# A hybrid decoder layer on one core: queries and first key/value columns of the in-projection by seven block products, compression moved into the convolution stage

## The chip, the cores and the metric

One core of one Trainium2 chip. The metric is the device time of one execution in microseconds (us). Engines: TensorE (PE, with its weight loads PEld), VectorE (DVE), ScalarE (ACT), GpSimd (POOL) and SyncE (SP), whose queue issues most transfers.

## The reference

One layer on x of 1024 tokens by 1024 columns, in fp32. A token mixer (sparse attention with three branches, and a gated short convolution) and an MLP:

```
h = rms_norm(x, g_mix_norm)
z = h @ w_in                                   # 1024 x 2840
q, kc, vc, ks, vs, kw, vw, gates, hc, cg, bg = split(z)
        # q 512 columns; kc, vc, ks, vs, kw, vw 128 each; gates 24; hc, cg, bg 512 each
k_cmp = rms_norm(gelu(blocks(kc) @ w_cmp1[0] + b) @ w_cmp2[0] + b)     # "compression"
v_cmp =          gelu(blocks(vc) @ w_cmp1[1] + b) @ w_cmp2[1] + b
attn  = gated sum of attention on (k_cmp, v_cmp), on selected blocks (ks, vs), in a window (kw, vw)
conv  = bg * causal_conv3(cg * hc)
x = x + [rms_norm(attn), rms_norm(conv)] @ w_o
x = x + square(relu(rms_norm(x) @ w_up)) @ w_down
```

## The kernel before

Every fp32 product is three passes of TensorE (`mm3`, L636): high times high, high times low, low times high. The high half of an operand is a copy by ScalarE (`copy_act`, L629), the low half a subtraction, mostly by VectorE. One matmul has a 128x128 stationary operand and 512 moving columns (280 or 256 in places) and sums into a bank of PSUM.

The stages, in the order of the program:

- **Front.** `x_in` (L748) loads x transposed in 16 pieces of 128x512 (256 KB), scales and splits them; `norm_in` loads x again for the norms of the tokens. `z_tokens` (L801) multiplies tokens (stationary) by columns of w_in: first 512 columns kc, vc, ks, vs of all eight token blocks, then the 512 columns of q, then 280 columns (kw, vw, gates). That is 8 (blocks of 128 rows of w_in) x 8 (token blocks) x 3 passes = 192 matmuls for each of the three; the first two together are the 384 of 512 columns. `token_sums` (L821) makes sums of blocks of x that the convolution stage needs, `late_sum` (L831) one more. Keys are normed (`k_norm`) and written to DRAM turned; q likewise.
- **Compression.** `compress_steps` (L880) is a generator; between the q matmuls one step at a time is taken: load the blocks of kc or vc from DRAM (`ch`), turn them (`tp`), split them (`ah`, `al`; the latter on POOL), load w_cmp1 in eight pieces (`w1r`), split each (`w1h`, `w1l`), 96 matmuls in all into `hp`, then gelu, a turn and the second product.
- **Convolution.** `channels` (L1054) already computes a 2x2 block product with seven products, not eight (Strassen's way in Winograd's form): A11, S1, S2, A12, S3, S4, A22, each with a block of x or a sum of such (`b11`, `t1`, `t2`, `b21`, `b12`, `b22`, `t4`), summed in three chains of banks X, W, Z. `u_pair` (L1092) and the loop after it evaluate them and convolve.
- **Output projection of the convolution part** (`wc` matmuls), keys, scores and values of the attention, the rest of w_o, and an MLP whose products are by seven as well.

All of this is recorded into `Plan` (L156) and written out at the end: a list scheduler (`schedule`, `latest`) gives each instruction a rank from the longest work behind it and orders each engine's queue; `shaken` (L565) shakes the ranks with the numbers in `SEEDS` (L153), and the best of its orders by its own costs is issued (`best`, `issue`). So all instructions have the line L273 of the issuing helper, and are told apart by tile names. `plan.plus`, `plan.slack`, `plan.drag` and `plan.follow` move the rank of single operations. PSUM has eight banks: three of the pool psP (L700; "pt") and five of psB (L702; "mm"). In each engine's queue instructions run in order; a transfer in SP's queue waits with all behind it until its tile is free.

Of the kernel before, what the change touches and what calls it, by code (L numbers as in the profile page):

```python
# [19 lines left out]
P = 128  # L20
# [4 lines left out]
H = 8  # L25
# [21 lines left out]
C_CONV = C_GATE + 3 * H  # L47
GELU_C = 0.7978845608028654
# [104 lines left out]
SEEDS = (174, 96, 16, 293, 242, 303, 622, 488, 681, 529, 552, 868, 906, 858, 745, 812, 849, 989, 1138, 1111, 1227, 1330, 1240, 1619, 1452, 1751, 1854, 1808, 1969, 2299, 2182, 2463, 2584, 3018, 3202, 4890, 5120, 5678, 5748, 5759, 5732, 5809, 5825, 6181, 6472, 6446, 6357, 6538, 6828, 7002, 7139, 7387, 7641, 7905, 7699, 8110, 8891, 9541, 9548, 9753, 9890, 10201, 10211, 10442, 12007, 13133, 13704, 13855, 13990, 15390, 15367, 15624, 15886, 16292, 16730, 16933, 17091, 17166, 17516, 17595, 17935, 17801, 17972, 18997, 19783, 20400, 21422, 23298, 24412, 24583, 24684, 25041, 25935, 26634, 27058, 30527, 37332, 43721, 44172, 45465, 56150, 69531, 71323, 73032, 73374, 78977, 79699, 84172, 87695, 92708, 93300, 98646, 99114, 99374, 120984, 125933, 126536, 137741, 144395, 147541, 152192, 155111, 155792, 163960, 208317, 212893, 221248, 221764,)  # L153


class Plan:  # L156
# [450 lines left out]
def trunk_layer(ctx, tc, x, x_t, vectors, w_in, g_qk, w_cmp1, b_cmp1, w_cmp2, b_cmp2,  # L607
# [79 lines left out]
    ht_stack = ExitStack()  # L687
    htp = pool(ht_stack, "htp")
    b_stack, wp_stack = ExitStack(), ExitStack()
    twp = pool(b_stack, "twp", side="right")  # L690
    hTh = [(twp, htp)[i].tile([P, KD, 512], F32R, name=f"hTh{i}") for i in range(2)]
    hTl = [(twp, htp)[i].tile([P, KD, 512], F32R, name=f"hTl{i}") for i in range(2)]

    kcn = twp.tile([P, 2 * HD], F32, name="kcn")
    g_bc = twp.tile([P, 4, HD], F32, name="g_bc")
    gq_bc, gk_bc = g_bc[:, 0], g_bc[:, 1:]
    TD = {n: [htp.tile([P, 4, 512], F32R, name=f"{n}{q}") for q in "hl"] for n in ("t1", "t2")}
    wp = pool(wp_stack, "wp", bufs=4, side="right")
    psP_stack = ctx.enter_context(ExitStack())
    psP = pool(psP_stack, "psP", bufs=3, space=PSUM, side="right")  # L700
    psB_stack = ExitStack()
    psB = pool(psB_stack, "psB", bufs=5, space=PSUM)  # L702

# [30 lines left out]
    b1 = ExitStack()
    zt = pool(b1, "zt", bufs=2, side="right")
    xp_stack = ExitStack()
    xp = pool(xp_stack, "xp", side="right")

    def quarter(i, j):
        return [a[j][:, 4 * i:4 * i + 4] for a in (hTh, hTl)]  # L740

    TD["b11"], TD["b12"], TD["b21"], TD["b22"] = quarter(0, 0), quarter(0, 1), quarter(1, 0), quarter(1, 1)

    def x_part(k, th):
        q = f"{k // 4 + 1}{th + 1}"
        return [xT[q][:, k % 4]] + [a[:, k % 4] for a in TD["b" + q]]

    def x_in(k, th):  # L748
        raw, hi, lo = x_part(k, th)
# [5 lines left out]

    def norm_in(tb):
        xt = xp.tile([P, D], F32, name="xt") if tb % 2 else zt.tile([P, D], F32, name="xt", tag="qn", bufs=1)
# [3 lines left out]
        rsqrt(rmix[:, tb:tb + 1], ss, 1, 1.0 / D)  # L761

    plan.plus = 200.0
    nc.scalar.dma_start(cols, vectors)
    tp = psP.tile([P, 512], F32, name="warm", tag="pt")
# [4 lines left out]
    kv_pieces, last = [], []  # L770
    for j in range(4):
        if j:
            for k in (2 * j, 2 * j + 1):
                x_in(k, 0)
            kv_pieces.append(w_piece(wiv[:, 2 * j:2 * j + 2, C_KV:C_KV + 512], [P, 2, 512], lo_eng=nc.vector))
            continue
        raw = wp.tile([P, 2, 512], F32, name="w_raw", bufs=2)
        kv_pieces.append((wp.tile([P, 2, 512], F32R, name="w_hi"), wp.tile([P, 2, 512], F32R, name="w_lo")))
        for k in range(2):
            x_in(k, 0)  # L780
            hi, lo = [a[:, k] for a in kv_pieces[0]]
            nc.sync.dma_start(raw[:, k], wiv[:, k, C_KV:C_KV + 512])
            if k:
                copy_act(hi, raw[:, k])
            else:
                nc.vector.tensor_copy(hi, raw[:, k])
            tt(nc.vector, lo, raw[:, k], hi.bitcast(F32), ALU.subtract)
    for tb in range(4):
        norm_in(tb)
    for k in range(KD):  # L790
        x_in(k, 1)
    for tb in range(4, NT):
# [6 lines left out]
    tt(nc.vector, gk_bc, gk_bc, gq_bc.unsqueeze(1).to_broadcast([P, 3, HD]), ALU.mult)  # L799

    def z_tokens(pieces, tbs, n, steps=iter(()), per=0):  # L801
        pss = [psB.tile([P, 512], F32, name="zp", tag="mm") for _ in tbs]
        for j, (wh, wl) in enumerate(pieces):
            for ps, tb in zip(pss, tbs):
                t = slice((tb % 4) * P, (tb % 4 + 1) * P)
                for i in range(2):
                    k = 2 * j + i
                    mm3(ps[:, :n], hTh[tb // 4][:, k, t], hTl[tb // 4][:, k, t], wh[:, i], wl[:, i],
                        k == 0, k == KD - 1)
            for _ in range(per):  # L810
                plan.plus = 12
                next(steps, None)
                plan.plus = 0.0
        return list(zip(tbs, pss))

    def split_sum(o, k, raw):
        hi, lo = [a[:, k] for a in TD[o]]
        copy_act(hi, raw)
        tt(nc.vector, lo, raw, hi.bitcast(F32), ALU.subtract)

    def token_sums():  # L821
        for k in range(4):
            x11, x12, x21, x22 = [xT[n][:, k] for n in ("11", "12", "21", "22")]
            tt(nc.vector, x11, x12, x11, ALU.subtract)
            split_sum("t1", k, x11)
            tt(nc.vector, x22, x22, x11, ALU.subtract)
            split_sum("t2", k, x22)
            tt(nc.vector, x21, x21, x22, ALU.subtract)
            split_sum("t4", k, x21)

    def late_sum(tp_, o, p, m):  # L831
        f = {n: [a.bitcast(F32) for a in TD[n]] for n in (m, p)}
        for k in range(4):
            (ah, al), (bh, bl) = [[a[:, k] for a in f[n]] for n in (m, p)]
            a, b = [tp_.tile([P, 512], F32, name=n, bufs=1) for n in ("ta", "tb")]
            tt(nc.vector, a, bh, ah, ALU.subtract)
            tt(nc.vector, b, bl, al, ALU.subtract)
            tt(nc.vector, a, a, b, ALU.add)
            split_sum(o, k, a)

    token_sums()
    with b1:
        def k_norm(src, br, tb):
            dst = zt.tile([P, 2, G, 32], F32, name="krow")
            sq = zt.tile([P, HD], BF16, name="ksq", bufs=2)
            ss = st.tile([P, G], F32, name="kss")
            for g in range(G):
                c = slice(g * HD, (g + 1) * HD)
                nc.scalar.activation(sq, src[:, c], AF.Square, accum_out=ss[:, g:g + 1])
            ri = st.tile([P, G], F32, name="kri")  # L850
            rsqrt(ri, ss, G, 1.0 / HD)
            for g in range(G):
                nc.vector.scalar_tensor_tensor(dst[:, :, g], src[:, g * HD:(g + 1) * HD].rearrange("p (j d) -> p j d", j=2),
                                               ri[:, g:g + 1], gk_bc[:, br].rearrange("p (j d) -> p j d", j=2),
# [1041 lines left out]
```

## Time and profile before

| | |
|---|---|
| median of 3 runs | 1188.5 us (1187.66 to 1188.91) |
| the profiled execution | 1187.4 us, its span 1185.6 us |
| busy share of the span | PE 99%, PEld 82%, DVE 77%, ACT 59%, POOL 61% |
| matmuls, transposes included | 5766 |
| instructions of DVE, ACT, POOL | 1827, 1550, 663 |
| read from and written to HBM | 111.87 and 48.23 MB |

How to read it: busy times are sums of single instructions. Matmuls overlap, so the duration of one (0.39 us for 512 columns) is longer than what it occupies TensorE; that is read from the starts of neighbours, or from how many start in a stretch. The granted clock (PEclk) is given in tenths of full speed; 9 is 90% or more.

### The profile page before, as it was taken

What the parts mean: (1) busy time and instruction counts of PE and PEld (TensorE: products, weight loads), DVE (VectorE), ACT (ScalarE), POOL (GpSimd) and SP (SyncE); (2) the same over time, 40 slices, a digit from 0 to 9 for tenths busy, and PEclk for the clock granted to TensorE, in tenths of its full rate; (3) what the DMA queues carried; (4) which work ended last, traced back from release to release, by engine and by line L of the source; (5) the groups of instructions that cost most, each with busy time, mean ns of one, the idle gap of its engine ahead of it and who ended that gap; (6) DMA issues with size and microseconds to landing.
All of it is one profiled execution on the core that took longest, in us unless ns stands there. A gap on an engine that the chain in (4) does not pass through costs nothing.

```text
span 1185.6 us, 18003 instructions
## 1 busy us (share of the span) xinstructions
PE 1173.6 (99%) x5766; PEld 977.4 (82%) x5766; DVE 908.0 (77%) x1827; ACT 698.3 (59%) x1550; POOL 722.9 (61%) x663
## 2 busy tenths in 40 slices
PE   9999999999999999999999999999999999999998
PEld 7888978888878888888788888888888888888887
DVE  8868968696799999998876555554479979887875
ACT  7868634362599988889764555546335444444441
POOL 1444400013356554535878977877799899888971
PEclk9999999999999999999999999999999999999999
DMA  9745581245121101104055535353469545553513
GB/s 341 194 138 169 154 153 50 68 162 171 53 64 46 61 12 63 55 19 143 18 178 186 167 127 187 121 182 121 163 230 389 149 137 178 162 167 102 174 46 142
DMA packets 115102, 161.28 MB, mean 136 GB/s; under 512 B 21472, under 2 KB 68960, under 8 KB 115008
## 3 DMA queue, kind: packets, MB, share of 16 engines
q1 hardware_dynamic: 108752, 152.44, 40.4%
q10 hardware_dynamic: 5520, 5.28, 1.3%
q0 software_dynamic: 736, 2.43, 0.7%
q8 instruction: 45, 0.74, 0.3%
q14 instruction: 49, 0.40, 0.1%
HBM read 111.87 MB, written 48.23 MB: 135 GB/s over the span
## 4 chain that ended last, share of the span: by engine, by line
PE 90%; DVE 4%; ACT 3%; DMA 1%; issue 1%; SPq 0%; ACTq 0%; DVEq 0%
PE X L273 29%; PE Z L273 18%; PE zp L273 8%; PE zX L273 5%; PE ot L273 5%; PE tp L273 5%; PE wc L273 4%; PE W L273 4%; PE wa L273 3%; PE zZ L273 3%; PE zW L273 1%; DVE pl L273 1%; DMA w1r<-in_w_cmp_dram 1%; DVE pt L273 1%; PE hp L273 1%
## 5 line engine op out<-in xcount | busy, mean ns | idle before, releaser
L273 PE MATMUL X<-we,uu 128*128 128x512 f32 (+1 forms) x726 | 201.0, 388 | 0.0
L273 PE MATMUL Z<-we,uu 128*128 128x512 f32 (+1 forms) x576 | 166.2, 388 | 0.0
L273 PEld LDWEIGHTS X<-we,uu 128*128 128x128 f32 x726 | 136.0, 188 | 28.2 <-DVE y L273 0.2
L273 ACT ACTIVATE uu<-ur 128x512 fp32r<-128x512 f32 x108 | 67.2, 630 | 123.4 <-PE Z L273 70.9
L273 PEld LDWEIGHTS Z<-we,uu 128*128 128x128 f32 x576 | 107.9, 188 | 22.3
L273 ACT ACTIVATE pt<-pt,nm 128x640 f32<-128x640 f32 (+7 forms) x128 | 93.7, 734 | 39.7 <-DVE nm L273 39.4
L273 DVE TENSOR_TENSOR y<-X,y 128x512 f32<-128x512 f32 x129 | 86.8, 682 | 32.5 <-PE X L273 31.4
L273 POOL TENSOR_TENSOR d<-d 128x512 f32<-128x512 f32 x64 | 98.0, 1551 | 9.9 <-DVE d L273 8.3
L273 DVE TENSOR_TENSOR pl<-tp,ph 128x512 fp32r<-128x512 f32 (+1 forms) x148 | 95.0, 654 | 3.6 <-ACT ph L273 3.2
L273 PE MATMUL tp<-ident,pt 128*128 128x128 f32 x528 | 91.2, 273 | 0.0
L273 ACT ACTIVATE ph<-tp 128x512 fp32r<-128x512 f32 (+1 forms) x148 | 80.8, 573 | 11.3 <-PE tp L273 8.9
L273 POOL TENSOR_TENSOR uu<-ur,uu 128x512 fp32r<-128x512 f32 x54 | 80.9, 1502 | 5.0 <-ACT uu L273 4.9
L273 ACT ACTIVATE we<-s 128x512 fp32r<-128x512 f32 x55 | 34.7, 631 | 83.6 <-PE Z L273 46.8
L273 DVE TENSOR_TENSOR y<-Z,y 128x512 f32<-128x512 f32 x96 | 64.9, 681 | 21.6 <-PE Z L273 21.2
L273 PEld LDWEIGHTS tp<-ident,pt 128*128 128x128 f32 x528 | 66.0, 141 | 10.7 <-DVE pl L273 0.6
L273 POOL MEMSET Qz<- 64x512 f32 x16 | 8.3, 520 | 106.0 <-PE zZ L273 104.5
L273 PE MATMUL zp<-w_hi,hTh 128*128 128x512 f32 (+1 forms) x192 | 64.6, 365 | 0.4 <-ACT hTh L273 0.4
L273 PE MATMUL zp<-w_lo,hTh 128*128 128x512 f32 (+1 forms) x192 | 64.8, 363 | 0.0
L273 PE MATMUL zp<-w_hi,hTl 128*128 128x512 f32 (+1 forms) x192 | 64.1, 360 | 0.0
L273 DVE TENSOR_TENSOR we<-wu,we 128x512 fp32r<-128x512 f32 x38 | 43.4, 1153 | 26.0 <-PE X L273 16.6
L273 POOL TENSOR_TENSOR we<-wd,we 128x512 fp32r<-128x512 f32 x32 | 48.0, 1501 | 24.7 <-ACT we L273 24.3
L273 POOL TENSOR_TENSOR pt<-pt,rr 128x640 f32<-128x640 f32 (+4 forms) x64 | 62.3, 1001 | 0.0
(1353 smaller groups left out, 3608.0 us busy)
## 6 DMA issues: line engine op xcount, KB each, us to landing
u_d<-d SPq DMA_DIRECT2D x112, 256.0 KB, 3.6
ur<-u_d SPq DMA_DIRECT2D x108, 256.0 KB, 2.8
wu<-in_w_up_dram SPq DMA_DIRECT2D x16, 1024.0 KB, 5.9
wd<-in_w_down_dram SPq DMA_DIRECT2D x16, 1024.0 KB, 6.9
xt<-in_x_dram SPq DMA_DIRECT2D x10, 512.0 KB, 5.6
x<-in_x_t_dram SPq DMA_DIRECT2D x16, 256.0 KB, 6.6
w1r<-in_w_cmp_dram SPq DMA_DIRECT2D x16, 256.0 KB, 2.8
q_d<-qn SPq DMA_DIRECT2D x8, 512.0 KB, 3.5
```

The lines of the kernel that those rows point to most:

```text
L273: node.do.append(lambda: getattr(engine, method)(*[real(x) for x in a], **{k: real(x) for k, x in kw.items()}))
```

## The change

The q columns (512) and the columns kc, vc, ks, vs (512) become the two halves of one 1024x1024 block product with the seven products of the convolution stage: weights A11, A12 (q and kv columns of the rows, in halves) and sums S1 to S4, tokens in the sums that the convolution needs anyway, all of which are now made at the start (`late_sum` goes). Each product is 4 x 4 x 3 = 48 matmuls; seven are 336 in place of 384. The 280 columns come first (`rest_tokens`). Compression is advanced inside the convolution's products (`advance`, two steps after each product from the third on), and what is left of it runs before the first output gate. The tiles of the convolution's output and the loads of keys (`kn`) move behind that. PSUM has, until the attention, four banks in rotation, one "m5" (compression's `hp`, `cps`, late chains W) and three of a pool ps0. New ranks: 152 numbers, some of which shake a narrower stretch.

```
-SEEDS = (174, 96, 16, 293, ...)
+SEEDS = (186, 36, 24000136, 238, 1000267, ...)
...
         a, w, size, how = r.uniform(0, 700), r.uniform(5, 40), r.choice((.5, 1, 2, 5)), r.random()
+        if seed >= 1000000:
+            a, w = seed // 1000000 * 10 + r.uniform(-5, 10), r.uniform(1, 15)
...
+    def bank(name, fifth=False):
+        return psB.tile([P, 512], F32, name=name, tag="m5" if fifth else "mm", bufs=1 if fifth else 4)
+    def banks(name, outer):
+        if not outer:
+            return [bank(name) for _ in range(4)]
+        return [ps0.tile([P, 512], F32, name=name, tag=t, bufs=n) for t, n in (("pt", 1), ("r2", 2), ("r2", 2))] + [bank(name, True)]
...
+    def rest_tokens(th):
+        pss = banks("zp", th == 0)
+        for k in range(KD):
+            bh, bl = TD[f"b{k // 4 + 1}{th + 1}"]
+            for j, ps in enumerate(pss):
+                t = slice(j * P, (j + 1) * P)
+                mm3(ps[:, :280], bh[:, k % 4, t], bl[:, k % 4, t], rest[0][:, k], rest[1][:, k], k == 0, k == KD - 1)
...
+    def product(name, b, chain, first, ready):
+        if first:
+            Z[chain] = banks("z" + chain, chain == "X")
+        bh, bl = TD[b]
+        for k in range(4):
+            ready(k)
+            raw = W[name, k]
+            hi, lo = [wr.tile([P, 512], F32R, name=f"w{q}", bufs=HL) for q in "hl"]
+            copy_act(hi, raw)
+            tt(nc.vector, lo, raw, hi.bitcast(F32), ALU.subtract)
+            if name == "S2":
+                a12 = W["S4", k] = W["A12", k]
+                tt(nc.gpsimd, a12, a12, raw, ALU.subtract)
+            for j, ps in enumerate(Z[chain]):
+                t = slice(j * P, (j + 1) * P)
+                mm3(ps, bh[:, k, t], bl[:, k, t], hi, lo, first and k == 0, k == 3, skip_group_check=True)
...
+    def sums_k(k):
+        a11, a21, a22 = W["A11", k], w_in_k("A21", 0, k, w_tile("c")), w_in_k("A22", 1, k, w_tile("d"))
+        tt(nc.vector, a11, a11, a21, ALU.subtract)
+        tt(nc.vector, a21, a21, a22, ALU.add)
+        tt(nc.vector, a22, a22, a11, ALU.subtract)
+        W["S3", k], W["S1", k], W["S2", k] = a11, a21, a22
...
+    product("A12", "b21", "W", True, lambda k: w_in_k("A12", 1, k, w_tile("b")))
+    t0 = kept("X", 0, x_tile, "t0")
+    product("S2", "t2", "X", False, sums_k)
+    for tb in range(4):
+        kv_out(tb, Z["W"][tb], t0[tb])
...
+    product("S1", "t1", "Z", True, lambda k: None)
+    t1 = kept("X", 1, w_tile("d"), "t1")
+    product("S3", "b12", "X", False, lambda k: None)
+    za = kept("Z", 1, w_tile("c"), "za")
+    product("S4", "b22", "Z", False, lambda k: None)
+    for tb in range(4, NT):
+        q_out(tb, Z["X"][tb - 4], za[tb - 4])
+    product("A22", "t4", "X", False, lambda k: w_in_k("A22", 1, k, w_tile("a")))
+    for tb in range(4, NT):
+        kv_out(tb, Z["Z"][tb - 4], t1[tb - 4])
+    wr_stack.close()
+    for tb in range(4):
+        q_out(tb, Z["X"][tb])
...
+        def advance():
+            done.append(None)
+            if len(done) > SKIP:
+                plan.plus = 12
+                for _ in range(STEPS):
+                    next(steps, None)
+                plan.plus = 0.0
...
                 if chain not in ps:
-                    ps[chain] = psB.tile([P, 512], F32, name="z" + chain, tag="mm")
+                    ps[chain] = bank("z" + chain, chain == "W" and len(done) > 14)
...
                 yield name, ps[chain]
+                advance()
...
+            if c == 0:
+                for _ in steps:
+                    pass
+                cp_stack.close()
+                zt_stack.close()
+                mcp = pool(b2, "mcp", side="right")
+                MCh, MCl = [mcp.tile([P, 4, T], F32R, name=f"MC{q}") for q in "hl"]
```

Counted over the whole program, TensorE has 48 matmuls 128x512 less and nothing else changed; VectorE has 30 operations on two tensors 128x512 more, 12 fused ones (scale and add), 8 of 280 columns, and 7 of 1024 and 4 of 560 columns less; ScalarE 27 of 512 and 8 of 280 more, 7 of 1024 and 4 of 560 less; POOL 4 subtractions 128x512 more; SP 18 transfers of 512 and 8 of 280 columns more, 7 of 2x512 and 4 of 2x280 less.

SP's queue at the start of the program, before (w_raw are columns kc to vs of w_in, x the transposed input):

```order
L273 DMA w_raw<-in_w_in_dram 128x512
L273 DMA x_184<-in_x_t_dram 128x512
L273 DMA w_raw<-in_w_in_dram 128x512
L273 DMA x_184<-in_x_t_dram 128x512
L273 DMA w_raw<-in_w_in_dram 128x2x512
```

and after (wk are rows of the 280 columns):

```order
L275 DMA x_162<-in_x_t_dram 128x512
L275 DMA x_163<-in_x_t_dram 128x512
L275 DMA x_164<-in_x_t_dram 128x512
L275 DMA x_165<-in_x_t_dram 128x512
L275 DMA wk<-in_w_in_dram 128x280 x2
L275 DMA x_166<-in_x_t_dram 128x512
```

A first weight piece and a first x piece were the first two transfers; now four x pieces precede the first weight piece.

VectorE's queue of the change around the first low half of A12 (wl_185, from wA12_308), with buffer numbers (x11 to x22 are blocks of x and their sums, wA11 and wA21 weights and their sums, t2l the low half of a sum, krow and kturn the keys of the window, g_bc the norm's factors):

```order
L275 TENSOR_TENSOR wA11_192<-wA11_192,wA21_370 128x512
L275 TENSOR_TENSOR t2l_642<-x11_162,t2h_469 128x512
L275 TENSOR_SCALAR rs_t_614<-kss_610 128x2
L275 TENSOR_SCALAR rs_t_593<-kss_579 128x2
L275 TENSOR_TENSOR x11_165<-x22_177,x11_165 128x512
L275 STREAM_TRANSPOSE kturn_773<-krow_671 128x128
L275 TENSOR_TENSOR x21_169<-x21_169,x11_165 128x512
L275 TENSOR_SCALAR gates_65<-ge_607 128x12
L275 TENSOR_TENSOR wl_185<-wA12_308,wh_190 128x512
L275 SCALAR_TENSOR_TENSOR krow_827<-z_650,kri_653,g_bc_207 128x2x32 x2
L275 TENSOR_TENSOR wl_804<-wA12_329,wh_808 128x512
```

Before, the second group of weights needed only its own split on VectorE; sums of x stood beside it and sums of weights did not exist. Now both stand ahead of the low half.

TensorE's queue where the compression's hidden products (hp, from pieces w1h, w1l and blocks ah, al) stand, before (zp are projection matmuls):

```order
L273 MATMUL zp<-w_lo,hTh_126 128x512
L273 MATMUL hp<-w1h,ah_742 128x256
L273 MATMUL hp<-w1l,ah_742 128x256
L273 MATMUL zp<-w_hi,hTh_126 128x512
L273 MATMUL zp<-w_lo,hTh_126 128x512
L273 MATMUL zp<-w_hi,hTl_125 128x512 x2
L273 MATMUL zp<-w_hi,hTh_126 128x512 x2
```

and after (zX, a chain of the convolution; r, the turn of the tokens' norm factors):

```order
L275 MATMUL zX<-b12l,wcuh 128x512
L275 MATMUL hp<-w1h,ah_1691 128x256
L275 MATMUL hp<-w1l,ah_1691 128x256
L275 MATMUL zX<-b12h,wcul 128x512
L275 MATMUL zX<-b12h,wcuh 128x512
L275 MATMUL r_1650<-ident,bc 128x128
L275 MATMUL hp<-w1h,al_1690 128x256
```

The hidden products have moved from among the projection's matmuls to among the convolution's.

## Rows read from the trace of the kernel before

**Rows 1.** The page: busy time, share and instructions of each engine; VectorE's busy tenths and the granted clock in 40 slices of the span.

```profile
PE 1173.6 (99%) x5766; PEld 977.4 (82%) x5766; DVE 908.0 (77%) x1827; ACT 698.3 (59%) x1550; POOL 722.9 (61%) x663
...
DVE  8868968696799999998876555554479979887875
...
PEclk9999999999999999999999999999999999999999
```

**Rows 2.** Busy time by stretch: the stretch, its length, then busy time and instructions started of PE, PEld, DVE, ACT and POOL, granted clock, share of the DMA engines, GB/s.

```profile
5.00:10.00 5.00, 4.58 (x19) 3.44 (x18) 3.31 (x6) 2.96 (x5) 0.00 (x0) 1.00 0.98 342
8.00:60.00 52.00, 51.98 (x224) 42.10 (x225) 46.63 (x100) 42.84 (x99) 18.32 (x27) 1.00 0.87 274
66.00:137.00 71.00, 69.14 (x436) 61.36 (x435) 58.22 (x127) 50.92 (x206) 34.36 (x29) 1.00 0.53 158
137.00:160.00 23.00, 22.27 (x104) 17.88 (x103) 19.08 (x55) 12.20 (x36) 7.85 (x10) 1.00 0.58 141
160.00:260.00 100.00, 100.00 (x438) 80.64 (x437) 79.72 (x127) 46.08 (x80) 4.78 (x9) 1.00 0.35 79
310.00:345.00 35.00, 32.45 (x191) 25.69 (x190) 34.65 (x110) 33.40 (x85) 17.23 (x27) 1.00 0.26 76
345.00:560.00 215.00, 214.93 (x1327) 185.70 (x1327) 200.91 (x679) 187.26 (x432) 117.49 (x184) 1.00 0.17 57
560.00:1180.00 620.00, 618.25 (x2752) 509.85 (x2751) 432.65 (x539) 302.66 (x559) 509.04 (x345) 1.00 0.47 158
```

**Rows 3.** The chain of work that ended last, in order of time: start, length, what (x: instructions in one piece).

```profile
8.02 58.46 PE zp L273 x251
66.83 0.76 PE tp L273 x7
...
96.17 0.60 PE hp L273 x5
...
117.30 4.63 PE zp L273 x36
...
257.75 5.74 PE wc L273 x24
```

**Rows 4.** Groups of TensorE's matmuls from 66 to 137 us, shapes apart: line, operation, output from inputs, shape, count, then busy time and mean ns of one, then idle time just before them and what ended it.

```profile
L273 PE MATMUL zp<-w_hi,hTl 128*128 128x512 f32 x45 | 16.7, 399 | 0.0
L273 PE MATMUL zp<-w_lo,hTh 128*128 128x512 f32 x43 | 16.4, 402 | 0.0
L273 PE MATMUL zp<-w_hi,hTh 128*128 128x512 f32 x42 | 16.1, 397 | 0.0
L273 PE MATMUL zp<-w_hi,hTh 128*128 128x280 f32 x59 | 15.3, 293 | 0.0
L273 PE MATMUL zp<-w_lo,hTh 128*128 128x280 f32 x59 | 15.2, 293 | 0.0
L273 PE MATMUL zp<-w_hi,hTl 128*128 128x280 f32 x57 | 14.4, 291 | 0.0
L273 PE MATMUL hp<-w1l,ah 128*128 128x256 f32 x32 | 9.2, 288 | 0.8 <-DVE w1l L273 0.6
L273 PE MATMUL hp<-w1h,ah 128*128 128x256 f32 x32 | 9.2, 287 | 0.9 <-ACT w1h L273 0.9
L273 PE MATMUL hp<-w1h,al 128*128 128x256 f32 x32 | 9.0, 281 | 0.0
L273 PE MATMUL tp<-ident,ch 128*128 128x128 f32 x16 | 2.9, 272 | 0.0
```

**Rows 5.** TensorE's instructions in order of time at the start: start, length, engine, instruction, count, and in brackets the idle time before it and what ended it (the first six projection matmuls, and the first of the unbroken run).

```profile
5.34 1.22 PE L273 MATMUL zp<-w_hi,hTh 128*128 128x512 f32 x2
...
7.21 0.39 PE L273 MATMUL zp<-w_hi,hTl 128*128 128x512 f32 x1
8.02 0.50 PE L273 MATMUL zp<-w_hi,hTh 128*128 128x512 f32 x1 [0.41 <-ACT hTh L273]
```

**Rows 6.** ScalarE's instructions in order of time: the splits of the first and second x piece.

```profile
4.57 0.72 ACT L273 ACTIVATE hTh<-x,cols 128x512 fp32r<-128x512 f32 x1 [1.87 <-DMA x<-in_x_t_dram]
...
7.24 0.72 ACT L273 ACTIVATE hTh<-x,cols 128x512 fp32r<-128x512 f32 x1 [1.43 <-DMA x<-in_x_t_dram]
```

**Rows 7.** VectorE's instructions in order of time, several of one kind on one row: the length is from the first's start to the last's end.

```profile
5.33 0.75 DVE L273 SCALAR_TENSOR_TENSOR hTl<-x,cols,hTh 128x512 fp32r<-128x512 f32 x1 [0.39 <-ACT hTh L273]
...
10.82 4.73 DVE L273 SCALAR_TENSOR_TENSOR hTl<-x,cols,hTh 128x512 fp32r<-128x512 f32 x7
15.45 1.28 DVE L273 TENSOR_SCALAR x<-x,cols 128x512 f32<-128x512 f32 x3
...
30.54 0.48 DVE L273 SCALAR_TENSOR_TENSOR krow<-z,kri,g_bc 128x64 f32<-128x64 f32 x2
...
33.39 1.89 DVE L273 TENSOR_TENSOR x<-x,x 128x512 f32<-128x512 f32 x3
```

**Rows 8.** Groups of VectorE's instructions from 160 to 260 us, columns as in rows 4: the low halves of the convolution's weights, and an evacuation of a chain X.

```profile
L273 DVE TENSOR_TENSOR wcul<-wcr,wcuh 128x512 fp32r<-128x512 f32 x29 | 19.7, 684 | 3.3 <-PE zX L273 1.6 <-PE zZ L273 1.2 <-ACT wcuh L273 0.5
...
L273 DVE TENSOR_TENSOR ca<-zX,ca 128x512 f32<-128x512 f32 x5 | 3.4, 690 | 10.5 <-PE zX L273 10.5
```

**Rows 9.** The page's costliest groups, columns as in rows 4: low halves of the MLP's weights on VectorE and on POOL.

```profile
L273 DVE TENSOR_TENSOR we<-wu,we 128x512 fp32r<-128x512 f32 x38 | 43.4, 1153 | 26.0 <-PE X L273 16.6
...
L273 POOL TENSOR_TENSOR we<-wd,we 128x512 fp32r<-128x512 f32 x32 | 48.0, 1501 | 24.7 <-ACT we L273 24.3
```

More of the change, by code (lines that the diff above doesn't have):

```diff
@@ L47 @@
 C_CONV = C_GATE + 3 * H
+HL = 5
+SKIP, STEPS = 2, 2
 GELU_C = 0.7978845608028654
@@ new lines, in kept @@
+    def kept(chain, th, tile, name):
+        out = []
+        for j, ps in enumerate(Z[chain]):
+            t = tile(name)
+            copy_act(t, ps, scale=rmix[:, 4 * th + j:4 * th + j + 1])
+            out.append(t)
+        return out
+    def sums_k(k):
[4 more added lines that the diff above has]
+        W["S3", k], W["S1", k], W["S2", k] = a11, a21, a22
@@ new lines, in k_norm @@
+    def k_norm(src, br, tb):
+        dst = zt.tile([P, 2, G, 32], F32, name="krow")
+        sq = zt.tile([P, HD], BF16, name="ksq", bufs=2)
+        ss = st.tile([P, G], F32, name="kss")
+        for g in range(G):
+            c = slice(g * HD, (g + 1) * HD)
+            nc.scalar.activation(sq, src[:, c], AF.Square, accum_out=ss[:, g:g + 1])
+        ri = st.tile([P, G], F32, name="kri")
+        rsqrt(ri, ss, G, 1.0 / HD)
+        for g in range(G):
+            nc.vector.scalar_tensor_tensor(dst[:, :, g], src[:, g * HD:(g + 1) * HD].rearrange("p (j d) -> p j d", j=2),
+                                           ri[:, g:g + 1], gk_bc[:, br].rearrange("p (j d) -> p j d", j=2),
+                                           op0=ALU.mult, op1=ALU.mult)
+        turned = zt.tile([P, G * HD], F32, name="kturn", bufs=1)
+        nc.vector.transpose(turned, dst.rearrange("p j g d -> p (j g d)"))
+        nc.sync.dma_start(k_d[br - 1][tb * P:(tb + 1) * P], turned)
@@ new lines, in q_out @@
+    def q_out(tb, ps, t=None):
+        z = zt.tile([P, 512], F32, name="z") if t is None else t
+        if t is None:
+            copy_act(z, ps, scale=rmix[:, tb:tb + 1])
+        else:
+            nc.vector.scalar_tensor_tensor(z, ps, rmix[:, tb:tb + 1], t, op0=ALU.mult, op1=ALU.add)
+        sq = zt.tile([P, HD], BF16, name="qsq", tag="ksq", bufs=2)
+        ss = st.tile([P, H], F32, name="qss", bufs=2)
+        for h in range(H):
+            c = slice(h * HD, (h + 1) * HD)
+            nc.scalar.activation(sq, z[:, c], AF.Square, accum_out=ss[:, h:h + 1])
+        ri = st.tile([P, H], F32, name="qri", bufs=2)
+        rsqrt(ri, ss, H, 1.0 / HD)
+        tt(nc.vector, ri, ri, qscale, ALU.mult)
+        qn = zt.tile([P, G, 4, R, 32], F32R, name="qn", bufs=1)
+        zh = z.rearrange("p (h d) -> p h d", h=H)
+        tt(nc.vector, zh, zh, ri.unsqueeze(2).to_broadcast([P, H, HD]), ALU.mult)
+        zT = zt.tile([P, 512], F32, name="zT", bufs=1)
+        nc.vector.transpose(zT, z)
+        for g in range(G):
+            zg = zT[:, g * 256:(g + 1) * 256].rearrange("p (r c t) -> p c r t", r=R, c=2)
+            hi, lo = qn[:, g, 2 * g:2 * g + 2], qn[:, g, 2 - 2 * g:4 - 2 * g]
+            copy_act(hi, zg)
+            tt(nc.vector, lo, zg, hi.bitcast(F32), ALU.subtract)
+        nc.sync.dma_start(q_d[tb * P:(tb + 1) * P], qn.rearrange("p g c r t -> p (g c r t)").bitcast(F32))
@@ L769, in trunk_layer @@
     plan.plus, plan.cold = 0.0, False
[L770 to L787, printed above, removed]
+    last = []
+    for k in range(KD):
+        x_in(k, 0)
+        rest_in(k)
     for tb in range(4):
[L789 to L792, printed above, removed]
         norm_in(tb)
@@ L799, in trunk_layer @@
     tt(nc.vector, gk_bc, gk_bc, gq_bc.unsqueeze(1).to_broadcast([P, 3, HD]), ALU.mult)
[L801 to L805, printed above, removed]
+    rest_tokens(0)
+    for k in range(KD):
+        x_in(k, 1)
+    for tb in range(4, NT):
+        norm_in(tb)
+    rest_tokens(1)
@@ new lines, in trunk_layer @@
+    for n in ("t2", "t1", "t4"):
+        operand(n)
+    product("A11", "b11", "X", True, lambda k: w_in_k("A11", 0, k, w_tile("a")))
+    for k in range(4):
+        x11, x12, x21, x22 = [X[n, k] for n in ("11", "12", "21", "22")]
+        tt(nc.vector, x22, x22, x12, ALU.subtract)
+        tt(nc.vector, x12, x12, x11, ALU.subtract)
+        tt(nc.vector, x11, x22, x11, ALU.add)
+        split_sum("t2", k, x11)
+        tt(nc.vector, x21, x21, x11, ALU.subtract)
+        split_sum("t1", k, x12)
+        split_sum("b12", k, x22)
+        split_sum("t4", k, x21)
@@ L806, in z_tokens @@
                 for i in range(2):
                     k = 2 * j + i
[L808 to L839, printed above, removed]
```

396 lines of the change are left out of this document (177 added, 219 removed).

## The prediction

> **What bounds the kernel now.** I read the busy times and the slices first, then busy times by stage, then the chain that ended last, and single instructions at last. TensorE is busy 99% of the span at full granted clock in every slice [rows 1]. So the time is the length of TensorE's queue, and what counts is how long each matmul occupies it, start to start, not its pipelined duration (0.39 us). By stage [rows 2]: from 8 to 60 us 224 matmuls of 512 columns start in 52.0 us, 0.232 each; from 160 to 260 us 438 in 100 us, 0.228 each. In both TensorE never stops. Two stages are looser. From 66 to 137 us, where the compression stands among the projection's matmuls, TensorE shows 1.9 us idle, and more is lost between starts (below). From 310 to 345 us, the start of the attention, it is idle 2.5 us while VectorE is busy 34.65 of 35. The MLP (560 to 1180) is TensorE alone. The chain says the same at the front: from 8.02 us on 251 projection matmuls without a break [rows 3]. VectorE has no slack from 10 to about 40 us and some in all later stages but the attention. The profiled execution took 1187.4 us, 1.1 under the median of 1188.5; the sum is made against the former and 1.1 is added.
>
> **The change part by part.**
> *Removed matmuls.* The orders differ on TensorE by 48 matmuls 128x512 and nothing else: seven products of 48 in place of 384. They stood in a stage that is nothing but TensorE: 48 x 0.232 = **-11.1 us** (at 0.228 it is 10.9).
>
> *Start.* Before, TensorE did six projection matmuls from 5.34 us on, then ran unbroken from 8.02, when the second x piece had been split [rows 5, 6]. It was the fourth transfer. After, the first weight piece (280 columns) is the fifth transfer, behind four x pieces; about 140 KB more at the 342 GB/s of that stretch [rows 2] is 0.4 us after the fourth piece at 7.2 (which ScalarE splits at 7.24), and a split of 280 columns follows (0.72 us for 512 [rows 6], so about 0.4). I take a first matmul at 8.5: 0.5 late, and the six (1.4 us) not done: **+1.9**. Ends: +0.5 if the piece comes with the fourth; +3 if splits of VectorE, which takes about 1.4 us for each k against TensorE's 1.55 (12 x 0.129), run late as well.
>
> *VectorE's backlog.* The sums of tokens, and new sums of weights, must be made for the same hour. In the new order 24 subtractions, 16 scaled splits, 16 scalings (512 columns), 8 splits of 280, 8 key rows and some two dozen small ones stand before and with the low half of A12, the first of the second product. Start to start these take 0.605, (4.73-0.75)/6 = 0.663, 0.40, 0.33 (0.605 x 280/512) and 0.24 us [rows 7], small ones 0.1 at most: 14.5+10.6+6.4+2.6+1.9+2.4 = 38.4. VectorE begins at 5.3 and loses 1.7 us before 10 us [rows 2, 7]: ready at 45.4. TensorE wants it after 192 matmuls of 280 columns (0.129 each [rows 3], 24.8 us) and 49 of 512 (11.4): at 44.7. **+1.0** with the step to the matmul. Ends: 0, and +8 if VectorE goes at the durations of single instructions (0.68 to 0.75) instead. I take the start-to-start times, since in this stretch before VectorE has run back to back. What is queued behind that low half are three more of A12 and the key rows of the window; TensorE waits only for the former, each 2.8 us apart.
>
> *The old 66 to 137 us.* 130 projection matmuls of 512, 175 of 280, 96 of 256 and 16 transposes start there [rows 4], with three of the next stage, four more transposes and twelve tiny ones. At 0.228, 0.129 [rows 3], 0.12 (five in 0.60 [rows 3]), 0.109 [rows 3] and 0.08 that is 30.3+22.6+11.5+2.2+1.0 = 67.6; the stage took 71.0 [rows 2]. 3.4 us were lost to splits of the compression's weights and to the mix. In the new order plain products stand here and the 280-column work comes first, in blocks: **-3.4** (end 0: the same losses elsewhere).
>
> *Compression in the convolution stage.* What moves: 96 matmuls of hidden products, transposes, 32 splits of its weights on ScalarE and VectorE, eight subtractions on POOL, 16 transfers of 256 KB, two of the second weights and four of the blocks on SP, four biases on POOL's queue. On SP's queue they are now behind the projection's pieces and among the convolution's weights; the loads of turned keys and of the first output weights, once ahead or beside, stand behind them. At 79 GB/s [rows 2] that stage has room. POOL is busy 4.8 of 100 us there [rows 2], so its subtractions (1.5 us [rows 9]) fit. VectorE: 98.8 us busy from 137 to 260, less 16 operations of late sums (9.7), plus some 20 of compression: 109 in about 137 us; it stays behind TensorE. The waits that stood before the hidden products (0.8 and 0.9 [rows 4]) I expect again: **+1.7**. Ends 0 and +5: the first pair's output waits for the end of the compression, since their tiles take its place.
>
> *Evacuations.* VectorE gains 30 operations of 512 columns and 12 fused scale-and-adds (25 and 8 us), seven large splits fall away. They lie in the products from 45 to 125 us, a stretch that some 20 us of compression leave and where VectorE was busy 58 of 71 us [rows 2]. Covered by TensorE's 48 matmuls (11.1 us) between two uses of a bank group: nothing; without that cover each group would cost up to four evacuations, 2.4 us.
>
> *Attention and MLP.* Same operations. The MLP at nothing: TensorE queues there whatever came before. The attention at nothing, ends -2.5 (its idle time [rows 2] gone) and +2.6 (as much again), since ranks are new.
>
> Sum: -11.1+1.9+1.0-3.4+1.7 = -9.9: 1177.5 on the profiled execution, **1178.6 us** on the median.
>
> **A rule against it.** The same kind of subtraction took VectorE 0.684 us in the convolution stage [rows 8], where POOL is nearly unused, and 1.15 in the MLP, where POOL does subtractions of 1.5 us beside it [rows 9]. The Trainium skill ("SBUF — State Buffer", on the shared port pair) states that an operation of VectorE with two SBUF inputs and one of GpSimd that reads SBUF lock each other out for a whole instruction. The trace agrees. The sum above goes without such locks, as in the convolution stage; by the rule the sum is that of rival A.
>
> **The rivals.**
> *A: POOL gets in VectorE's way.* The change gives POOL four new subtractions (A12 less S2) right where VectorE makes the splits of S2, and eight more of compression in the convolution stage. If each blocks VectorE for 0.5 us (1.15 less 0.684) up to 1.5, twelve of them cost VectorE 6 to 18 us; TensorE feels it only where VectorE is the later, at the backlog above and S2. I price it at 6, the low end: **1184.6**. For it: the MLP's rows. Against: POOL is busy 18 of the 52 us from 8 to 60 us [rows 2], and VectorE ran back to back beside that; later VectorE has slack.
>
> *B: the gain is taken back in the attention.* VectorE is busy 34.65 of 35 and 200.9 of 215 us there [rows 2]; if VectorE's queue, not TensorE, decides when it can end, an earlier start becomes waiting. **1187.5**, about no change. Against: TensorE shows no idle time from 345 to 560, so it is level with VectorE, and to lose all ten it would need four times the idle time of 310 to 345.
>
> *C: slower, by banks.* The convolution stage has four banks in rotation and a fifth that the compression holds, where it had five. Each of six calls takes three for chains X, W and Z, so at the five hand-overs 15 banks must have been read before the next chain starts. If an evacuation on VectorE comes 0.9 us late each time, 15 x 0.9 = 13.5 us are lost: **1192**. It decides from 0.82 us on (12.3 us, the gain and the bound below). For it: VectorE is busy 80%, and queue order, not need, says when the evacuation runs. Against: a chain X is 48 matmuls, 10.9 us, and in five waits for such a chain VectorE idled 10.5 us [rows 8].
>
> That the change doesn't do what it says is excluded by the count of 48.
>
> **How the numbers follow.** Within 0.2% (2.4 us) a measurement of this kernel can't be told from no change. Chances: forecast 0.64, A 0.18, B 0.09, C 0.09. Forecast and A are faster by more than that: 0.82; B the same: 0.09; C slower: 0.09. The forecast's own range is 1172 to 1182: down by the attention's 2.5, an earlier start (1.4), no backlog and no compression loss (2.7); up by the start's 1.1 and the compression's 3.3, less a part. With A and half of B the range is **1172 to 1187**; C and the backlog's +8 with other losses stay out.
>
> **What would show it.** Right: the first projection matmul at about 8.5 us, a gap of about 1 us before the second product at 45; 0.23 us a matmul in the products; the convolution stage giving way to the output projection 9 to 11 us before the 258 us of before [rows 3]; TensorE's idle time in 310 to 345 unchanged. Wrong: gaps over 3 us at S2 with VectorE's lows at 1.1 us or more (A); a front that ends ten earlier and an attention that is ten longer (B); gaps before each first matmul of a chain, released by VectorE (C); or starts of the 280-column block more than 0.14 us apart.

## The result and the profile after

The changed kernel takes 1177.96 us (median of 4 runs, 1177.56 to 1178.41), the kernel before on the same chip 1188.08 us: a ratio of 0.9916, 95% interval 0.9898 to 0.9933. The forecast was 1178.6 us. On another chip the changed kernel took 1178.87 us beside 1187.18 of the kernel before, ratio 0.9930 (0.9915 to 0.9945). The gain is 8 to 10 us. One execution of 4172 us among eleven of a kernel below (product S1 doubled) is left out of its ratio.

Busy times, VectorE's tenths and the granted clock of the page after, which answer to [rows 1]:

```profile
PE 1162.9 (99%) x5718; PEld 968.6 (82%) x5718; DVE 927.2 (79%) x1865; ACT 703.4 (60%) x1574; POOL 733.3 (62%) x667
...
DVE  7988998794899999998976555554578879878875
...
PEclk8999999999999999999999999999999999999999
```

TensorE's busy time fell by 10.7 us, the 48 matmuls. VectorE has 19 us more. The first slice of the clock is no longer full.

Stretches of the changed kernel, columns as in [rows 2]:

```profile
5.00:10.00 5.00, 1.58 (x7) 1.55 (x7) 3.93 (x9) 3.63 (x7) 0.00 (x0) 0.76 1.00 307
8.00:14.00 6.00, 5.55 (x24) 5.55 (x25) 5.96 (x14) 4.88 (x11) 0.00 (x0) 0.50 1.05 366
20.00:66.00 46.00, 46.00 (x255) 39.96 (x254) 43.77 (x107) 37.14 (x107) 23.99 (x27) 1.00 0.58 201
44.00:70.00 26.00, 26.00 (x115) 20.85 (x114) 25.72 (x52) 19.53 (x63) 13.56 (x14) 1.00 0.30 84
66.00:120.00 54.00, 54.00 (x233) 43.41 (x232) 46.98 (x117) 39.05 (x173) 25.51 (x29) 1.00 0.57 161
66.00:137.00 71.00, 71.00 (x321) 57.55 (x320) 61.87 (x142) 53.67 (x225) 30.95 (x32) 1.00 0.62 172
130.00:180.00 50.00, 48.79 (x262) 40.69 (x261) 48.25 (x81) 29.11 (x67) 17.30 (x14) 1.00 0.51 146
137.00:160.00 23.00, 21.79 (x115) 17.80 (x114) 21.28 (x43) 12.61 (x25) 7.75 (x7) 1.00 0.49 148
300.00:335.00 35.00, 33.30 (x193) 26.44 (x191) 33.65 (x108) 32.22 (x78) 17.38 (x28) 1.00 0.25 76
```

From 20 to 137 us TensorE never stops; the 1.9 us of idle time that [rows 2] show from 66 to 137 us are gone. But VectorE is busy 25.72 of 26 us from 44 to 70 and 48.25 of 50 from 130 to 180 us. That it is level with TensorE in two places is what the experiments below turn on.

The start, in order of time, which answers to [rows 5]:

```profile
8.45 1.30 PE L275 MATMUL zp<-resth,b11h 128*128 128x280 f32 x4 [3.42 <-ACT resth L275]
9.55 0.43 PE L275 MATMUL zp<-restl,b11h 128*128 128x280 f32 x1
9.79 0.43 PE L275 MATMUL zp<-resth,b11l 128*128 128x280 f32 x1
...
14.45 0.30 PE L275 MATMUL zp<-restl,b11h 128*128 128x280 f32 x1
14.59 0.29 PE L275 MATMUL zp<-resth,b11l 128*128 128x280 f32 x1
```

The first projection matmul comes at 8.45 us (forecast 8.5). But TensorE had stood idle for 3.4 us, the granted clock is 0.50 from 8 to 14 us, the lower of the two levels (1.2 of 2.4 GHz), and matmuls of 280 columns start 0.233 us apart, not 0.129, until 14.4 us. That is one of the prediction's own signs of being wrong (starts of this block more than 0.14 us apart), for the first 25 matmuls of it.

The chain that ended last, which answers to [rows 3]:

```profile
8.45 21.48 PE zp L275 x144
...
250.48 4.84 PE wc L275 x21
```

The output projection of the convolution begins in earnest at 250.5 us, 257.75 before: the front is 7.3 us shorter. What follows takes 1175.9 - 250.5 = 925.4 us, before 1185.6 - 257.75 = 927.9.

### The profile page after: what moved, and what is told of

It reads as the page before. It is cut to its first block, busy times and chain, and to the rows that moved or that the text cites. A ratio compares the mean times of both kernels' runs of the same rounds, so it can differ in the third digit from the quotient of the medians.

```text
span 1175.9 us, 18035 instructions
## 1 busy us (share of the span) xinstructions
PE 1162.9 (99%) x5718; PEld 968.6 (82%) x5718; DVE 927.2 (79%) x1865; ACT 703.4 (60%) x1574; POOL 733.3 (62%) x667
## 4 chain that ended last, share of the span: by engine, by line
PE 92%; DVE 3%; ACT 2%; DMA 1%; issue 1%; SPq 0%; DVEq 0%
PE X L275 28%; PE Z L275 18%; PE zX L275 9%; PE tp L275 5%; PE zZ L275 5%; PE ot L275 5%; PE wc L275 4%; PE W L275 4%; PE wa L275 3%; PE zp L275 2%; PE zW L275 2%; DVE pl L275 1%; PE hp L275 1%; DVE pt L275 1%; DMA ur<-u_d 1%
## 5 line engine op out<-in xcount | busy, mean ns | idle before, releaser
L275 PEld LDWEIGHTS X<-we,uu 128*128 128x128 f32 x726 | 136.0, 188 | 28.8 <-DVE uu L275 0.6
L275 PE MATMUL tp<-ident,pt 128*128 128x128 f32 x528 | 95.0, 272 | 0.0
L275 DVE TENSOR_TENSOR we<-wu,we 128x512 fp32r<-128x512 f32 x38 | 51.1, 1360 | 21.8 <-PE X L275 12.8
L275 ACT ACTIVATE we<-wu 128x512 fp32r<-128x512 f32 x57 | 35.4, 628 | 46.4 <-PE X L275 32.6
L275 POOL TENSOR_TENSOR s<-wu 128x512 f32<-128x512 f32 x29 | 44.9, 1552 | 19.1 <-DVE we L275 14.7
L275 ACT ACTIVATE wu<-wu,cols 128x256 f32<-128x256 f32 x128 | 56.5, 500 | 0.0
L275 ACT ACTIVATE we<-wd 128x512 fp32r<-128x512 f32 x64 | 39.9, 628 | 26.9 <-PE X L275 13.9
```

The source lines that it names most:

```text
L275: node.do.append(lambda: getattr(engine, method)(*[real(x) for x in a], **{k: real(x) for k, x in kw.items()}))
```

## The experiments

All twelve runs stood beside the kernel before on the same chip. Ratios are to that.

**What 48 matmuls cost.** With each matmul of product S1 issued twice in the same order:

```
             for n in order:
-                for f in n.do:
-                    f()
+                for _ in range(getattr(n, "times", 1)):
+                    for f in n.do:
+                        f()
...
+                plan.times = 1 + (name == "S1")
                 mm3(ps, bh[:, k, t], bl[:, k, t], hi, lo, first and k == 0, k == 3, skip_group_check=True)
+                plan.times = 1
```

> The changed kernel in the same order, with each matmul of product S1 issued twice: 48 matmuls of 512 columns more (its sums are doubled). Theory (TensorE's queue alone sets the time there): 48 x 0.227 to 0.232 = 10.9 to 11.1 us more, 1188.9 us; no more idle time, since all else has it easier. Rival (VectorE, its evacuations or transfers set part of the pace, so TensorE has slack that the extra work fills): 5 to 9 us more, 1183 to 1187.

1188.62 us, ratio 1.0005 (0.9996 to 1.0014). The changed kernel stands at 0.9916 and 0.9930; the difference is 0.0075 to 0.0089 of 1188, 8.9 to 10.6 us. The convolution's last matmul starts at 259.6 us, 250.0 without. Added matmuls in that stretch pass through nearly in full, as the theory had it; whether matmuls taken out there would be gained, this does not show. The same trick was then used the other way.

**The compression's matmuls left out.** 84 of the 96, in the same order:

```
+plan.times = int(k in (0, 15))
 mm3(hp[:, :256], ah[:, k % 8], al[:, k % 8], wh[:, i], wl[:, i], k == 0, k == 15)
+plan.times = 1
```

> The changed kernel in the same order without 84 of the 96 hidden matmuls of the compression (keys and values of the compressed branch come out wrong); all splits, transfers and the first and last matmuls stay. Theory (in the convolution stage they stand in a queue that TensorE works through without waiting): 84 x 0.118 = 9.9 us less, 1168 to 1169, and no more than 1 us beyond that. Rival (they wait for pieces there as they did before): 11 to 13 us less.

> The kernel before in the same order without the same 84 matmuls. Theory (beside their 9.9 us they cost it 1.7 us of waits for pieces and part of the 3.4 us lost from 66 to 137 us): 11 to 13 us less, 1175 to 1177, which is 1 to 3 us more than the changed kernel gains by it. Rival (the losses of that stretch come from the mix and from VectorE's chain, not from these): 9.9 us less, 1178.

Both theories and both rivals missed. Without them the changed kernel takes 1178.07 us, ratio 0.9919 (0.9906 to 0.9933), within 1.3 us the same as with them, and the kernel before 1185.87 us, 0.9988 (0.9979 to 0.9997): 1.4 us less, not 10. Two stretches of the changed kernel without them, then one of the kernel before without them:

```profile
66.00:120.00 54.00, 54.00 (x233) 43.45 (x232) 46.31 (x116) 38.73 (x172) 25.20 (x28) 1.00 0.62 170
130.00:180.00 50.00, 42.08 (x184) 31.22 (x184) 48.37 (x84) 28.85 (x66) 16.98 (x14) 1.00 0.48 136
```

```profile
66.00:137.00 71.00, 63.47 (x353) 55.60 (x352) 56.02 (x125) 50.55 (x206) 34.53 (x29) 0.93 0.54 158
```

From 130 to 180 us TensorE's busy time falls from 48.8 to 42.1 us, and VectorE's stays at 48.4 of 50. TensorE now waits where it worked. Its largest waits there are for low halves, which VectorE makes (engine, tile, what released it: us in all, times, longest):

```profile
PE zZ L275 <- DVE wcul L275: 2.2, 2, 1.7
PE zX L275 <- DVE wcul L275: 1.7, 2, 1.0
PE hp L275 <- DVE w1l L275: 1.7, 2, 1.0
```

In the kernel before, TensorE is idle 7.5 of the 71 us in place of 1.9; three waits there are the largest:

```profile
PE zp L273 <- ACT w_hi L273: 2.9, 1, 2.9
PE tp L273 <- DVE hx L273: 2.6, 1, 2.6
PE hp L273 <- ACT w1h L273: 1.6, 1, 1.6
```

That is 5.6 us more of waiting. The rest of the 9.9 us went to the clock: it is 0.93 in that row (1.00 before), at the lower level from 91.1 to 94.4 and from 111.6 to 118.3 us, around those waits; (1 - 0.93) x 71 = 5.0 us is an estimate of its price. This profiled execution, 1187.81 us, is the slowest of eleven (1184.68 to 1187.81).

So in the changed kernel VectorE's queue is as long as TensorE's in the compression's stretch. In the kernel before no engine is full there (VectorE 56.0, ScalarE 50.6 of 71 us): single waits, for two splits by ScalarE and for the gelu, took back over half of what was left out, and the clock that fell with them most of the rest. TensorE's 99% don't tell either.

**POOL beside VectorE (rival A).** The four subtractions A12 less S2, each issued three times.

```
+plan.times = 3
 tt(nc.gpsimd, a12, a12, raw, ALU.subtract)
+plan.times = 1
```

> The changed kernel in the same order, with each of POOL's four subtractions (A12 less S2) issued three times, so 8 x 1.6 = 12.7 us more of POOL beside VectorE's splits and sums of weights (the sum S4 comes out wrong). In the changed kernel these VectorE operations took 0.77 us each from 44 to 70 us (21 of them), not 0.68, and TensorE lost nothing there. Theory (POOL does hold up VectorE, but the splits stand far enough ahead of TensorE): VectorE's mean goes up to 0.9 or more in that stretch, TensorE loses under 1 us, 1178 to 1180. Rival A (VectorE's backlog is on TensorE's path there): 8 x 0.5 to 8 x 1.5 us of VectorE reach TensorE, 4 to 10 us slower, 1182 to 1189.

1185.92 us, ratio 0.9986 (0.9977 to 0.9995): 0.0056 to 0.0070 over the changed kernel, 6.7 to 8.3 us slower for 12.7 us of POOL. The theory fell, the rival's price held. One stretch with three times the subtractions, and TensorE's waits from 44 to 80 us:

```profile
20.00:66.00 46.00, 42.90 (x234) 36.18 (x232) 44.73 (x102) 36.41 (x105) 29.16 (x30) 1.00 0.58 202
```

```profile
PE zX L275 <- ACT wh L275: 3.1, 2, 2.0
PE zX L275 <- DVE wl L275: 2.0, 2, 1.5
```

VectorE's groups from 44 to 70 us in the changed kernel and then with three times the subtractions, columns as in [rows 4]:

```profile
L275 DVE TENSOR_TENSOR wA<-wA,wA 128x512 f32<-128x512 f32 x11 | 8.4, 775 | 0.3
L275 DVE TENSOR_TENSOR wl<-wA,wh 128x512 fp32r<-128x512 f32 x10 | 7.7, 771 | 0.0
```

```profile
L275 DVE TENSOR_TENSOR wA<-wA,wA 128x512 f32<-128x512 f32 x10 | 9.9, 1002 | 0.2
L275 DVE TENSOR_TENSOR wl<-wA,wh 128x512 fp32r<-128x512 f32 x7 | 6.8, 971 | 0.0
```

```profile
66.00:80.00 14.00, 11.88 (x43) 9.24 (x44) 13.97 (x18) 7.50 (x24) 10.35 (x8) 0.88 0.22 53
```

The last fence is the stretch after, with three times the subtractions: VectorE is full with 18 instructions, and TensorE loses 2.1 of 14 us, after 3.1 of 46 before it; the clock is 0.88 there, which is worth (1 - 0.88) x 14 = 1.7 us. Together these are 6.9 us, the price. The waits go back to VectorE: the high halves come from ScalarE, but that waited 7.2 us from 44 to 80 us for VectorE's sums of weights. VectorE's operations went from 0.77 to about 1.0 us. In the changed kernel itself the effect is there, (0.773 - 0.684 [rows 8]) x 21 = 1.9 us of VectorE, and TensorE lost none of 46 us beside it: it is just covered. The Trainium skill's rule ("SBUF — State Buffer", on the shared port pair) agrees with this in kind: VectorE's operations with two inputs in SBUF slow (small ones with one, 128x2, did too, from 0.16 to 0.43 us on the average).

**The low clock at the start.** 28 more warm-up transposes close the gap before 8.45 us; run twice, the second time beside the changed kernel itself on one chip.

```
 for n in order:
     for f in n.do:
-        f()
+        for _ in range(29 if n is warm[-1] else 1):      # warm: the 19 warm-up transposes
+            f()
```

> The changed kernel with 28 more warm-up transposes ahead of the first projection matmul; nothing else moves. In the changed kernel TensorE stands idle from 5.0 to 8.45 us, its granted clock falls to 0.50, and the first 25 matmuls start 0.233 us apart instead of 0.129. Theory (the idle time costs the clock, and the clock costs time): clock 1.00 throughout, first projection matmul still at 8.4 to 8.5, later ones 0.129 apart until the fourth weight piece (split at 13.3 us) is awaited; about 15 matmuls more are done by 15.3 us, so the end is 2.0 us earlier, 1176 us (1175.4 if nothing is awaited: 25 x 0.104 = 2.6). Rival (pieces and VectorE set the pace of the first 15 us, so that the low clock hides): less than 0.5 us, 1177.5 to 1178.

> The changed kernel itself once more, as the control for the next one on the same chip. 1177 to 1179 us. The granted clock from 8 to 14 us says whether the low clock of the first profile (0.50) belongs to the kernel or to that chip: with an idle time of under 2.5 us ahead of the first projection matmul I expect 1.00, with over 3 us 0.50.

> The kernel with 28 more warm-up transposes again, beside the changed kernel on the same chip. Theory left after the first look (an earlier front is given back in the attention, where VectorE sets the pace): its front is up to 1.7 us ahead where the changed kernel's clock falls, and the end is within 0.6 us of it. Rival (it is worth what the front gains, and the chips differed): 1.5 to 2 us faster than the changed kernel.

1178.52 us, ratio 0.9917 (0.9904 to 0.9931); then 1178.75 beside 1178.87 us of the changed kernel: no difference. The clock was 1.00 with the transposes, and the products began earlier: X at 28.1 and 28.8 us in place of 29.8. The convolution's last matmul stood at 249.2 and 249.9 us, 250.0 and 250.1 without. A gain of 1.0 to 1.7 us at 28 us is 0.2 to 0.8 at 250: half of it or more goes before the attention (TensorE is idle 0.5 and 0.9 us from 20 to 137 us, where the changed kernel never is). What was left was gone at the end: behind that matmul the profiled executions took 927.3 and 928.7 us, 925.9 and 926.5 without, the longest of them with a clock of 0.95 from 300 to 335 us. So the theory on record for the second run, that the attention takes it, holds for a part at most. The rival of the first run had the number, but not the reason: the front did gain. On the chip of the control the idle time ahead of the first matmul was again 3.5 us, and 21 matmuls of 280 columns filled 4.85 us, 0.23 each:

```profile
8.00:14.00 6.00, 4.85 (x21) 4.86 (x22) 5.82 (x12) 5.30 (x11) 0.00 (x0) 1.00 1.00 342
```

The clock of 1.00 in this row is no reading. The trace of this execution holds no value of the clock before 13.75 us, and a stretch without one counts as full. The starts change from 0.23 to 0.13 us apart just there:

```profile
12.11 0.43 PE L275 MATMUL zp<-restl,b11h 128*128 128x280 f32 x1
12.34 0.43 PE L275 MATMUL zp<-resth,b11l 128*128 128x280 f32 x1
...
14.02 0.29 PE L275 MATMUL zp<-restl,b11h 128*128 128x280 f32 x1
14.14 0.29 PE L275 MATMUL zp<-resth,b11l 128*128 128x280 f32 x1
```

So the low clock belongs to the kernel, not to a chip, as was expected for an idle time over 3 us. The other half of that expectation did not hold: without the compression's matmuls the idle time was 2.2 us, and the clock 0.72 from 8 to 14 us.

**What the picked ranks are worth.** Both kernels without any shaking, and the changed one with only the numbers that shake a part of it:

```
-SEEDS = (186, 36, 24000136, 238, 1000267, ...)
+SEEDS = ()          # or the 30 for before 100 us, the 40 for 150 to 300 us, or those 70
```

> The changed kernel with no shaking of the ranks: the planner's own order. Together with the kernel before treated likewise it shows what the change is worth without ranks that were picked. Theory (the matmuls, the start and the compression's place give 8 us at the front; 2 more come from ranks in the attention): this one is slower than the changed kernel by 5 to 20 us, and 7 to 9 us faster than the kernel before without shaking. Rival (most of the 10 us is picked ranks): the two differ by less than 4 us.

> The kernel before with no shaking of the ranks. Theory: 5 to 20 us slower than the kernel before, and 7 to 9 us slower than the changed kernel without shaking. Rival (most of the 10 us is picked ranks): within 4 us of the changed kernel without shaking.

1199.81 us (1.0101, 1.0087 to 1.0115) and 1194.69 us (1.0057, 1.0044 to 1.0069), on one chip. In the planner's own order the change is 5.1 us slower, which neither theory had. Shaking brings the kernel before 6.8 us and the changed one 21 to 22. In its front alone the convolution's last matmul stands at 264.3 us unshaken and 250.0 with the picks (before: 256.8 and 257.4). The largest single wait of TensorE there, and VectorE's queue ahead of it, unshaken:

```profile
PE zX L275 <- DVE wcul L275: 3.3, 1, 3.3
```

```profile
253.71 1.81 DVE L275 TENSOR_TENSOR cv<-cv,c 128x512 f32<-128x512 f32 x2
255.44 2.39 DVE L275 TENSOR_TENSOR MCl<-cv,MCh 128x512 fp32r<-128x512 f32 x3
257.76 1.88 DVE L275 TENSOR_TENSOR sqs<-sqs,cv 128x512 f32<-128x512 f32 x3
259.56 0.68 DVE L275 TENSOR_TENSOR wcul<-wcr,wcuh 128x512 fp32r<-128x512 f32 x1
```

```profile
250.00:260.00 10.00, 6.47 (x28) 4.59 (x26) 9.36 (x14) 6.85 (x11) 4.54 (x8) 0.97 0.27 91
260.00:270.00 10.00, 9.08 (x34) 7.17 (x34) 5.79 (x11) 3.55 (x9) 0.00 (x0) 0.69 0.42 154
```

The low half that the last product needs stands behind eight operations, none of which that product needs. TensorE waits 3.3 us, and then its clock is 0.69 in the mean of 10 us: 13 matmuls of 512 columns start 0.43 us apart until 266 us, 0.23 after, which costs 13 x 0.20 = 2.6 us.

> The changed kernel with only those 30 of 152 rank numbers that shake stretches beginning before 100 us. Without any, TensorE lost 5.7 us between 20 and 66 us, waits for low halves of A11 and A12 among them, 7.4 us between 250 and 270, and the rest in attention and MLP; 1199.8 us in all. Theory (the first loss is VectorE's queue of sums and splits, put right by the early numbers alone): 5 to 7 us of it come back, 1193 to 1195. Rival (picks act only together): less than 3 us.

> The changed kernel with only those 40 rank numbers that shake stretches beginning from 150 to 300 us. Theory (a low half of the last A22 weights stood behind 8 us of evacuations on VectorE; TensorE waited 3.3 us, and its clock fell to 0.69 for the next 10 us): 6 to 8 us come back, 1192 to 1194, no wait over 1 us at the hand-over to the output projection and clock 1.00 there. Rival (that wait is a result of the late front, and goes only with it): less than 3 us.

> The changed kernel with the 70 rank numbers of both parts, before 100 us and from 150 to 300 us. The parts alone brought 6.3 and 9.7 us of the 21.9 that all 152 bring. Theory (two separate places on VectorE's queue, so the parts add): 1183 to 1185; the other 82 numbers, mostly of the attention, are worth 5 to 7 us. Rival (the places depend on each other): 1187 to 1190.

1193.49 us, 1190.12 us and 1186.35 us (ratios 1.0052, 1.0022 and 0.9992). These runs stand on other chips than the unshaken kernel; by ratios the gains below are 0.3 to 0.6 us smaller. The early numbers bring 6.3 us, as expected; those around the hand-over 9.7, more than expected, and the clock stays up there:

```profile
240.00:270.00 30.00, 30.00 (x142) 24.63 (x141) 27.80 (x50) 16.24 (x30) 7.89 (x12) 1.00 0.60 207
```

Together they bring 13.5, less than their sum and less than forecast. Nor do the parts add in the front: alone they move the convolution's last matmul from 264.3 to 256.5 and 254.9 us, 7.8 and 9.4, together to 250.2, 14.1. But that is all that the 152 numbers bring there. What is missing to the changed kernel lies behind: 7.5 us in attention and MLP, for the other 82 numbers.

## Why the prediction was right, and where it was not

**The removed matmuls (-11.1)**: right in size, as far as is shown; doubling a product cost 8.9 to 10.6 us, and TensorE's busy time fell by 10.7.

**Start (+1.9)**: the time of the first matmul was right, the term was too small. The idle time ahead of it let the clock fall, and 25 matmuls lost 25 x (0.233 - 0.129) = 2.6 us. The sum had the six matmuls not done, and not what a pause does to those after it. Taking the low clock away did not shorten the kernel, so the 2.6 can't be booked against the end in full either: at 250 us 0.2 to 0.8 of it was left.

**VectorE's backlog (+1.0)**: TensorE lost nothing from 20 to 66 us, and the gap of about 1 us before the second product did not come. The forecast that VectorE would be ready at about the time that it is wanted held: it is busy 25.72 of 26 us from 44 to 70, and 12.7 us more of POOL beside it delay the end by about 7.

**The old 66 to 137 us (-3.4)**: TensorE is busy 71.00 of 71. That these losses came from the mix is only argued: without the hidden matmuls they grew.

**Compression in the convolution stage (+1.7)**: 1.2 us idle from 137 to 160 (0.7 before [rows 2]), in waits of 0.3 for a low half and 0.9 for the gelu. The size is near; the reason given, that VectorE would stay behind TensorE at 109 in 137 us, is the step that failed. A mean of 80% hid 50 us at 97%.

**Attention and MLP (0)**: 2.5 us shorter in the profiled execution (925.4 for 927.9), 1.9 in the control's (1176.6 - 250.6 = 926.0). Of that 0.85 is idle time at the attention's start (1.70 of 35 us, 2.55 before [rows 2]), which was forecast unchanged. It lies in the bound of 2.5 and, in part, in what executions differ by.

So the front gave 7.3 of the 9.9 us, where 9 to 11 were to show the forecast right, and the rest 2.5: two errors of one size and opposite signs. That the sum came within 1 us is in part luck. With the low clock booked in full, no backlog and the compression as measured the front's sum is -11.1 + 1.9 + 2.6 - 3.4 + 1.2 = -8.8; with the 0.2 to 0.8 that was left of it at 250 us, -11.2 to -10.6. What the other 1.5 to 3.9 us are is left open.

**What was wrong in the argument**: "the time is the length of TensorE's queue". Downwards it holds only where no other chain is as long. The 48 added matmuls stand where VectorE has room (46.98 of 54 us from 66 to 120), and cost nearly their length. The compression's 84 stand in the changed kernel where it has none (48.25 of 50 us from 130 to 180), and counted for 1.3 us at most. In the kernel before they stood where no engine was full (VectorE 58.22 of 71 us [rows 2]), and counted for 1.4 us all the same: how full the next engine is does not tell it alone. The removed 48 were not tried by themselves; that they counted is read from the change, in which TensorE's busy time fell by 10.7 us and the time by 8 to 10. And the planner's order without picked ranks would have made rival C's side true, by 5.1 us, though not by banks: by VectorE's queue order at the hand-over and at the second product. The prediction named that ("queue order, not need, says when the evacuation runs") and had no evidence on how the new order stood. **Rival A** was there in kind and covered. **Rival B** didn't come: a later front moved the end by about as much (S1 doubled: 9.6 us at the convolution's last matmul, 8.9 to 10.6 at the end), and an earlier one too (the picks for 150 to 300 us moved the convolution's end by 9.4 us and the kernel's by 9.7).

Not tried: whether taking VectorE's work out of 130 to 180 us lets the low clock's and the hidden matmuls' time through, which the above would have happen.

## What to carry to other kernels

A 99% busy engine bounds a kernel from below; before removing work from it, look in that very stretch, not in the stage's mean, at how full the next engine is, and at what the first one would wait for then: single waits, and the clock that falls with them, took the gain back where no engine was full. Issuing an instruction twice or not at all in an unchanged order tells on a chip which of the two it is. A change that loads a second engine must be judged with an order made for it: here the same program stood 5 us behind or 10 us ahead by ranks alone.

## What the runs showed of the hardware that was not expected

TensorE's pauses cost more than their length: after 3.4 us without a matmul the granted clock stood at 0.50 from 8 to 14 us, after 3.3 us in the unshaken kernel at 0.69 in the mean from 260 to 270, and with 5.6 us more of waits in the kernel before it was 0.93 over 71 us. A clock of 1.00 can also mean that the trace has no value: in the control's profile it read so while matmuls of 280 columns started 0.23 us apart, so the starts are the surer sign at the start of a trace. And POOL's subtractions of 1.6 us beside them slowed VectorE's operations of two inputs from 0.68 to 0.77 us on the average, and to 1.0 as they became more.
